# Retention projections as Strassen blocks, with weight sums made in DRAM by transfers and the heads' outputs projected at the end

## The chip, the cores and the metric

One core of one Trainium2 chip. The metric is the device time of one execution in microseconds, as the median of several. The operands are float32; TensorE (PE) multiplies them as pairs of a rounded high part and a remainder ("hi" and "lo", type float32r), three matmuls for one: hi x hi, hi x lo, lo x hi. PE takes matmuls in the order in which they stand in its queue, as the other engines do with theirs.

## The reference

Two layers over 528 tokens (16 learned ones and 512 of the input) of width 1024. Layer 0 is retention and a SwiGLU FFN, layer 1 a gated DeltaNet and another FFN. The change is in the retention, which is, for 4 heads (q and k 256 wide, v and gate 512 wide):

```python
proj = h @ w_in                        # q, k, v, g of all heads
q = rope(q, pos); k = rope(k, pos)
scores = einsum("bhid,bhjd->bhij", qc, kc) * dmask
o = scores @ vc + (qc * xi) @ state    # chunkwise, with a decaying state
o = o * rsqrt(mean(o * o) + eps) * gn_w * silu(g)
h = h + o @ w_out
h = h + swiglu(rmsnorm(h, ffn_norm_w), w_gate, w_up, w_down)
```

The kernel works without chunks: it forms all scores of a head with the decay as a mask.

## The kernel before

Everything is kept transposed: `h` holds 8 tiles of 128 features by 528 tokens (`KT` = 8, `T` = 528), and a projection multiplies a 128x128 block of weights, held fixed in PE, with 264 columns of tokens, twice for the two halves. A tile of 128 outputs takes 8 such blocks x 3 matmuls x 2 halves = 48 matmuls (`gemm`, `mm3`, line 308). Weights come as 128x1024 float32 (512 KB) through the SP queue into `wraw`, and ScalarE (ACT) and VectorE (DVE) split them into `whi` (line 165) and `wlo` (line 166).

`retention` goes head by head: four tiles of q and k, rotated by `rope` (DVE, lines 425 to 427, split at 298 and 299) as soon as each pair of tiles is there; four tiles of v; four of the gate g; and four weight tiles of the projection of the head's output (`out_proj`), which runs among the next head's q and adds to `h` (line 417). So each head has 16 weight tiles and 768 matmuls of 264 columns. Scores (`ret_scores`), the transposition of v by token (`ret_values`) and the attending (`ret_attend`) are generators that `tick` takes a step further after every few matmuls of a projection, so that they stand among them in PE's queue. The normalisations run through `row_rsqrt`: squares summed by tiny matmuls (lines 390, 392), DVE makes `rc` (397), GpSimd (POOL) takes the power -1/2 (398), PE spreads it over partitions (401, 405), ACT copies it to `rb` (409, 410).

The FFNs do most of their first projections as Strassen blocks already (`forms`, `strassen`): a 2x2 block product with seven products in place of eight. `forms` makes seven combinations of the activations (names `fhb11` and so on, high and low), and `strassen` makes the weight sums on DVE (lines 275 to 286 and 269) before each product is split and multiplied.

The order on each engine is set by a scheduler: it lists each engine's instructions by the program's priority and by when it takes them to be ready. What it made of the change is shown below, with the change.

Of the kernel before, what the change touches and what calls it, by code (L numbers as in the profile page):

```python
# [14 lines left out]
P = 128  # L15
D = 1024
# [15 lines left out]
FORM = 3  # L32
PLAIN = 4
# [12 lines left out]
class Hybrid:  # L46
# [58 lines left out]
    def setup(self):  # L105
# [16 lines left out]
        for half in range(2):  # L122
            c = slice(half * 512, half * 512 + 512)
            nc.sync.dma_start(self.h[:, half, :], a["hT"][half])
            nc.sync.dma_start(self.first_w[0][:, c], a["w_qk"][0, 0, :, c])
# [4 lines left out]
        for kt in range(2, KT):  # L130
            nc.sync.dma_start(self.h[:, kt, :], a["hT"][kt])
            if kt == 4:
                nc.sync.dma_start(self.first_w[1], a["w_qk"][0, 1])
# [49 lines left out]
    FORMS = ("b11", "t1", "t2", "b22", "t3", "b21", "t4")  # L183

    def forms(self, st, fp, lo, hw):
# [6 lines left out]

        for k0 in (0, 2):
            f = self.t(fp, [P, 6 * hw], "wsum")
            a, b, c = (f[:, 2 * hw * i : 2 * hw * (i + 1)].rearrange("p (a b) -> p a b", a=2) for i in range(3))

            def block(dst, n, k0=k0):
                kb, half = 4 * (int(n[0]) - 1) + k0, int(n[1]) - 1
                cs = slice(lo + half * hw, lo + half * hw + hw)
                for k in range(2):  # L200
                    nc.vector.scalar_tensor_tensor(
                        dst[:, k, :], hh[:, kb + k, cs], g[:, kb + k : kb + k + 1], rb[:, cs], op0=ALU.mult, op1=ALU.mult
                    )

# [9 lines left out]
            yield FORM  # L214
            parts("b11", a)
            block(c, "22")
            yield FORM
            minus(a, b, a)
            parts("t1", a)
            minus(b, c, b)  # L220
            yield FORM
            minus(a, c, a)
            parts("b22", c)
            yield FORM
            parts("t2", a)
            block(c, "21")
            yield FORM
            parts("t3", b)
            minus(a, c, a)
            yield FORM  # L230
            parts("b21", c)
            parts("t4", a)
            yield FORM

    def quad(self, src, sp):
# [7 lines left out]
    def strassen(self, raw, st, sp, hw, out):  # L243
# [34 lines left out]
        nc.vector.tensor_tensor(s, s, raw["11"], op=ALU.subtract)  # L278
        product(s, "t2", xb, False)
        c22 = taken(zs)  # L280
        nc.vector.tensor_tensor(s, raw["12"], s, op=ALU.subtract)  # L281
# [4 lines left out]
        nc.vector.tensor_tensor(raw["21"], raw["11"], raw["21"], op=ALU.subtract)  # L286
# [152 lines left out]
    def ret_scores(self, rp, dp, hd, q, k, km, out):  # L439
# [4 lines left out]
        nc.gpsimd.dma_start(dm[:96], a["decm"][:, hd, :])  # L444
        dr = self.t(dp, [P, NT], "dr")
        nc.gpsimd.dma_start(dr, a["decr"][:, hd, :])
# [5 lines left out]
        for c0, c1 in ((NM, T), (0, NM)):  # L452
# [11 lines left out]
            sc = self.t(dp, [P, NT], "sc")  # L464
# [5 lines left out]
        for j in range(4):  # L470
# [12 lines left out]
            sc = self.t(dp, [P, NT], "sc")  # L483
# [7 lines left out]
    def ret_values(self, rp, hd, x, rb, ready):  # L491

        nc, a = self.nc, self.a
        vhi = self.t(rp, [P, 4, 512], "vhi", F32R)
        vlo = self.t(rp, [P, 4, 512], "vlo", F32R)
        vm = self.t(rp, [P, 512], "vm", F32R)

        def by_token(v, vt):
# [16 lines left out]
        steps = []  # L515
        for v in range(4):
            w = ready.pop(0) if ready else self.load_w(a["w_v"][hd, v])
            p = self.psum_g()
            self.gemm(p, w, x, range(KT))
            vt = self.t(self.tp, [P, T], "ra", bufs=4)  # L520
            nc.vector.tensor_tensor(self.halves(vt), self.flat(p), self.halves(rb), op=ALU.mult)
            steps.append(self.spawn(by_token(v, vt), VT))
        steps.append(self.spawn(meta(), VT + 1))
        return (vhi, vlo, vm), steps

    def ret_attend(self, rp, v3, sc, oraw, out, steps):
# [6 lines left out]
        oacc = self.t(rp, [P, T], "oacc")  # L533
# [22 lines left out]
    def retention(self, st, ctx, nxt):  # L556
        nc, a = self.nc, self.a
        x = (st["hi"], st["lo"])
        rp = self.pool(ctx, "ret", 1)
        dp = self.pool(ctx, "retd", 2)  # L560
# [5 lines left out]

        def begin():
            for kt in range(KT):
                self.norm_square(st, kt)
                yield 1  # L570
                if kt == 3:
                    nc.sync.dma_start(cosr, a["cos"])
                    nc.sync.dma_start(sinr, a["sin"])
# [3 lines left out]
            yield 1  # L577

# [5 lines left out]
        left = lambda: None  # L584
        for hd in range(RH):
            qk = {}
            raw = []
            oraw = self.t(rp, [P, 4, T], "oraw") if hd == 0 else None
            for i, nme in enumerate("qk"):
                if hd + i == 0:  # L590
                    first = [self.psum_g() for half in range(2)]
                    self.gemm_pair(first, w0, x)
                for half in range(2):
                    if hd + i == 0:
                        p = first[half]
                    else:
                        w = self.load_w(a["w_qk"][hd, 2 * i + half])
                        p = self.psum_g()
                        self.gemm(p, w, x, range(KT))
                    p = p[:, :, :HH]  # L600
                    if hd == 0:
                        keep = self.halves(oraw[:, 2 * i + half, :])
                        nc.scalar.copy(keep, p)
                        p = keep
                    raw.append(p)
                    if i == 0 and half == 0:
                        left()
                hi = self.t(rp, [P, 2, T], nme + "hi", F32R)
                lo = self.t(rp, [P, 2, T], nme + "lo", F32R)
                qk[nme] = (hi, lo)  # L610
                if hd > 0:
                    self.rope(hi, lo, raw[2 * i], raw[2 * i + 1], cosr, sinr)
            ready = []
            if hd == 0:
                ready = [self.load_w(a["w_v"][0, v]) for v in range(2)]
                self.finish(rows)
                rb = st["rb"]
                for i, nme in enumerate("qk"):
                    self.rope(*qk[nme], raw[2 * i], raw[2 * i + 1], cosr, sinr)
            sc = {}  # L620
            scores = self.spawn(self.ret_scores(rp, dp, hd, qk["q"], qk["k"], km, sc), SCORES[hd > 0])
            v3, steps = self.ret_values(rp, hd, x, rb, ready)
            self.finish(scores)
            if hd == 0:
                self.late_consts()
            else:
                oraw = self.t(rp, [P, 4, T], "oraw")
            orow = {}
            attend = self.spawn(self.ret_attend(rp, v3, sc, oraw, orow, steps), TO_ATTEND)
            ohi = self.t(rp, [P, 4, T], "ohi", F32R)  # L630
            olo = self.t(rp, [P, 4, T], "olo", F32R)

            def gated(v, sg, oraw=oraw, orow=orow, ohi=ohi, olo=olo):
                nc.vector.scalar_tensor_tensor(
                    oraw[:, v, :], oraw[:, v, :], self.gnw[:, v : v + 1], orow["rb"], op0=ALU.mult, op1=ALU.mult
                )
                nc.vector.tensor_tensor(sg, sg, oraw[:, v, :], op=ALU.mult)
                self.split(ohi[:, v, :], olo[:, v, :], sg)

            sgs = []  # L640
            for v in range(4):
                w = self.load_w(a["w_g"][hd, v])
                p = self.psum_g()
                self.gemm(p, w, x, range(KT))
                sg = self.t(self.tp, [P, T], "ra", bufs=4)
                nc.vector.tensor_tensor(self.halves(sg), p[:, :, :HH], self.halves(rb), op=ALU.mult)
                nc.scalar.activation(sg, sg, AF.Silu)
                sgs.append(sg)
                if v == 1:
                    self.finish(attend)  # L650
                if v > 0:
                    gated(v - 1, sgs[v - 1])
            gated(3, sgs[3])

            def out_proj(hd=hd, og=(ohi, olo), nst=None):
                for mp in range(4):
                    w = self.load_w(a["w_ro"][hd, mp])
                    for mi in range(2):
                        p = self.psum_g()
                        self.gemm(p, w, og, range(4), off=mi * 512)  # L660
                        self.add_h(p, 2 * mp + mi)
                        if nst:
                            self.norm_tile(nst, 2 * mp + mi)

            left = out_proj
        nst = nxt()
        out_proj(nst=nst)
        return nst

    def ffn_hidden(self, layer, st, lo, fp, up, name):  # L670
# [13 lines left out]
        for jp in range(PLAIN // 2):  # L684
            raw = self.quad(a["w_gu"][layer, jp], up)
# [40 lines left out]
        for jp in range(PLAIN // 2, FT // 2):  # L726
            raw = self.quad(a["w_gu"][layer, jp], up)

            def out(row, half, gate, u, jp=jp):
# [5 lines left out]
                nc.scalar.activation(s, gate, AF.Silu)  # L735
                own = j - 2 * KT + PLAIN
                dst = s if own >= PLAIN else late[j // KT][:, j % KT, cs]
                nc.vector.tensor_tensor(dst, s, u, op=ALU.mult)
# [706 lines left out]
def _layout(v):  # L1445
# [16 lines left out]
    q, k = blocks(w[:, :1024]), blocks(w[:, 1024:2048])  # L1462
    o["w_qk"] = c(np.concatenate([q.reshape(RH, 2, P, D), k.reshape(RH, 2, P, D)], axis=1))
    o["w_v"] = c(blocks(w[:, 2048:4096]).reshape(RH, 4, P, D))
    o["w_g"] = c(blocks(w[:, 4096:]).reshape(RH, 4, P, D))
    o["w_ro"] = c(
# [75 lines left out]
```

## Time and profile before

| what | us |
|---|---|
| median of 3 executions (1735.25 to 1739.01) | 1735.62 |
| the profiled execution | 1738.03 |
| its span, first to last instruction | 1736.2 |
| PE busy (matmul) | 1712.2 |
| DVE busy | 1138.5 |
| ACT busy | 802.6 |
| POOL busy | 74.6 |

The profile comes from one execution. A row of the timeline or of the chain gives start, duration, engine, line, operation and operands (out<-in), and how often; what is in brackets is the idle time before and what ended it. PE's matmuls overlap a little, so the spacing between them, not the length of one, is what a stretch costs. A row of a window gives its length and each engine's busy time with the number of instructions, then PE's granted clock, the busy share of the 16 transfer engines, and GB/s.

### The profile page before, as it was taken

What the parts mean: (1) busy time and instruction counts of PE and PEld (TensorE: products, weight loads), DVE (VectorE), ACT (ScalarE), POOL (GpSimd) and SP (SyncE); (2) the same over time, 40 slices, a digit from 0 to 9 for tenths busy, and PEclk for the clock granted to TensorE, in tenths of its full rate; (3) what the DMA queues carried; (4) which work ended last, traced back from release to release, by engine and by line L of the source; (5) the groups of instructions that cost most, each with busy time, mean ns of one, the idle gap of its engine ahead of it and who ended that gap; (6) DMA issues with size and microseconds to landing.
All of it is one profiled execution on the core that took longest, in us unless ns stands there. A gap on an engine that the chain in (4) does not pass through costs nothing.

```text
span 1736.2 us, 30593 instructions
## 1 busy us (share of the span) xinstructions
PE 1712.2 (99%) x12671; PEld 1598.5 (92%) x12671; DVE 1138.5 (66%) x1789; ACT 802.6 (46%) x1451; POOL 74.6 (4%) x138
## 2 busy tenths in 40 slices
PE   9999999999999999999999999999999999999997
PEld 8999999999999999999989978787877889999886
DVE  6555455554798777633588786685858798887322
ACT  5322322323444544523465526765666545445422
POOL 1000000000000000000030000000001000000010
PEclk9999999999999999999999999999999999999999
DMA  6222122221323322333255453433322223333221
GB/s 200 85 74 96 62 86 74 69 78 61 118 68 107 98 98 86 101 89 92 94 189 164 128 160 124 149 98 113 108 91 86 97 77 117 100 98 98 97 96 62
DMA packets 78747, 177.32 MB, mean 102 GB/s; under 512 B 19296, under 2 KB 36880, under 8 KB 78608
## 3 DMA queue, kind: packets, MB, share of 16 engines
q1 hardware_dynamic: 70704, 170.87, 30.7%
q0 software_dynamic: 944, 2.66, 0.5%
q10 hardware_dynamic: 6960, 1.84, 0.5%
q8 instruction: 99, 1.62, 0.4%
q14 instruction: 40, 0.33, 0.1%
HBM read 157.50 MB, written 17.84 MB: 101 GB/s over the span
## 4 chain that ended last, share of the span: by engine, by line
PE 87%; DVE 5%; issue 5%; ACT 2%; DMA 1%; POOL 0%; SPq 0%; POOLq 0%; ACTq 0%; DVEq 0%
PE g L308 72%; PE m L308 9%; DVE wlo L299 1%; DVE wlo L166 1%; DVE ra L799 1%; DMA sraw<-in_w_gu_dram 1%; PE m L405 1%; DMA h<-in_hT_dram 0%; ACT whi L298 0%; PE m L1124 0%; PE m L502 0%; PE m L392 0%; PE m L948 0%; ACT whi L165 0%; PE m L1225 0%
## 5 line engine op out<-in xcount | busy, mean ns | idle before, releaser
L308 PE MATMUL g<-xhi,whi 128*128 128x264 f32 (+1 forms) x1600 | 377.9, 305 | 1.3 <-ACT xhi L361 1.3
L308 PE MATMUL g<-xhi,wlo 128*128 128x264 f32 (+1 forms) x1600 | 366.0, 299 | 2.0 <-DVE wlo L166 2.0
L308 PE MATMUL g<-xlo,whi 128*128 128x264 f32 (+1 forms) x1600 | 365.8, 299 | 1.2 <-DVE xlo L362 1.2
L165 ACT CAST whi<-wraw 128x1024 fp32r<-128x1024 f32 (+1 forms) x176 | 181.1, 1030 | 378.6 <-PE g L308 308.0
L166 DVE TENSOR_TENSOR wlo<-wraw,whi 128x1024 fp32r<-128x1024 f32 (+1 forms) x176 | 210.7, 1199 | 163.5 <-ACT whi L165 159.0
L308 PEld LDWEIGHTS g<-xhi,whi 128*128 128x128 f32 x1600 | 256.9, 189 | 12.3 <-ACT xhi L361 2.0
L308 PEld LDWEIGHTS g<-xhi,wlo 128*128 128x128 f32 x1600 | 256.1, 189 | 10.7 <-DVE wlo L166 2.2
L308 PEld LDWEIGHTS g<-xlo,whi 128*128 128x128 f32 x1600 | 256.1, 189 | 8.7 <-DVE xlo L362 2.0
L308 PE MATMUL g<-fht,whi 128*128 128x264 f32 (+1 forms) x576 | 163.8, 284 | 0.2 <-DVE ra L269 0.2
L308 PE MATMUL g<-fht,wlo 128*128 128x264 f32 (+1 forms) x576 | 162.7, 282 | 0.6 <-DVE wlo L299 0.6
L308 PE MATMUL g<-flt,whi 128*128 128x264 f32 (+1 forms) x576 | 163.2, 283 | 0.0
L308 PEld LDWEIGHTS g<-fht,wlo 128*128 128x128 f32 x576 | 109.0, 189 | 0.9 <-DVE wlo L299 0.9
L308 PEld LDWEIGHTS g<-fht,whi 128*128 128x128 f32 x576 | 108.1, 188 | 0.9 <-issue 0.6
L308 PEld LDWEIGHTS g<-flt,whi 128*128 128x128 f32 x576 | 108.2, 188 | 0.0
L299 DVE TENSOR_TENSOR wlo<-wsum,whi 128x1024 fp32r<-128x1024 f32 x54 | 66.1, 1225 | 37.6 <-ACT whi L298 37.6
L298 ACT CAST whi<-wsum 128x1024 fp32r<-128x1024 f32 x54 | 56.6, 1048 | 72.7 <-DVE wsum L281 33.8
L308 PE MATMUL g<-fhb,wlo 128*128 128x264 f32 (+1 forms) x288 | 81.4, 283 | 0.5 <-DVE wlo L299 0.5
L308 PE MATMUL g<-fhb,whi 128*128 128x264 f32 (+1 forms) x288 | 81.8, 284 | 0.0
L308 PE MATMUL g<-flb,whi 128*128 128x264 f32 (+1 forms) x288 | 81.6, 283 | 0.0
L799 DVE SCALAR_TENSOR_TENSOR ra<-pad,convw,ra 128x528 f32<-128x528 f32 x96 | 75.4, 786 | 5.7 <-ACT ra L797 4.9
L417 DVE TENSOR_TENSOR h<-h,g 128x528 f32<-128x528 f32 x40 | 28.1, 703 | 53.0 <-PE g L308 53.0
L298 ACT CAST whi<-sraw 128x1024 fp32r<-128x1024 f32 x44 | 46.2, 1050 | 34.3 <-PE g L308 32.0
(397 smaller groups left out, 3721.9 us busy)
## 6 DMA issues: line engine op xcount, KB each, us to landing
wraw<-in_w_gu_dram SPq DMA_DIRECT2D x44, 512.0 KB, 3.3
sraw<-in_w_gu_dram SPq DMA_DIRECT2D x44, 512.0 KB, 3.5
wraw<-in_w_d_dram SPq DMA_DIRECT2D x38, 512.0 KB, 3.5
wraw<-in_w_v_dram SPq DMA_DIRECT2D x16, 512.0 KB, 3.3
wraw<-in_w_g_dram SPq DMA_DIRECT2D x16, 512.0 KB, 3.4
wraw<-in_w_ro_dram SPq DMA_DIRECT2D x16, 512.0 KB, 3.4
wraw<-in_w_dqk_dram SPq DMA_DIRECT2D x16, 512.0 KB, 3.4
wraw<-in_w_dv_dram SPq DMA_DIRECT2D x16, 512.0 KB, 3.4
```

Source lines behind the costliest of these rows:

```text
L165: nc.scalar.copy(hi[:, c], raw[:, c])
L166: nc.vector.tensor_tensor(lo[:, c], raw[:, c], hi[:, c].bitcast(F32), op=ALU.subtract)
L298: self.nc.scalar.copy(hi, src)
L299: self.nc.vector.tensor_tensor(lo, src, hi.bitcast(F32), op=ALU.subtract)
L308: mm(o, l, r[which], start=first and n == 0, stop=last and n == 2, **kw)
L405: nc.tensor.matmul(pr[:, j * P : (j + 1) * P], rc[:, j + 1 : j + 2].to_broadcast([P, P]), self.ident, start=True, stop=True)
L417: self.nc.vector.tensor_tensor(hs, hs, ps[:, :, :HH], op=ALU.add)
L799: nc.vector.scalar_tensor_tensor(acc, pad[:, i : i + T], cw[:, mt, i : i + 1], acc, op0=ALU.mult, op1=ALU.add)
```

## The change

Of the twelve projections of 1024 outputs (four heads; q with k, v, and g), nine become blocks of seven products (`quad`). Three stay plain (`plain`): q with k of head 0 and the gates of heads 0 and 1, which run first, while `forms` makes the seven combinations of the normalised activations. The gates of heads 0 and 1 go to DRAM (`d_sg`) until they are wanted.

The sums of weights that the blocks need are made before their use in DRAM. `sums` issues, on GpSimd's queue, plain copies and transfers that add to what stands at their destination (`accum_op=ALU.add`, in pieces of 1024 bytes): eight of 512 KB per block, 72 in all, each add behind the copy that it builds on. Because a transfer can only add here, signs move from the weight sums into the activations (`neither` in `forms`) and the results, in the FFNs too, where the sums stay on DVE. `all_sums` issues a step of it every 8 ticks from the moment the row factor `rb` of the first normalisation is there: a tiny transfer from `rb` to each `s1` puts that in order.

A block's outputs are gathered in SBUF. There is no room beside the combinations, so the first normalised activations (`xhi`, `xlo`) and `h` itself serve as space after `forms`, `h` is loaded again from its input, the heads' gated outputs go to DRAM (`d_o`) and come back, and their projection runs at the end over all four heads, in two passes of four output tiles, each followed by the next norm's `norm_tile`. The tables dm and dr, which GpSimd fetched, now come through SP.

```diff
-    def forms(self, st, fp, lo, hw):
+    def forms(self, st, fp, lo, hw, temp=None, pause=None):
...
+    def sums(self, w, s):
+
+        dma = self.nc.gpsimd.dma_start
+        dma(s["s1"], w[1])
+        dma(s["s3"], w[0])
+        yield
+        dma(s["s1"], w[2], accum_op=ALU.add, max_dma_last_dim=ROW)
+        dma(s["s3"], w[1], accum_op=ALU.add, max_dma_last_dim=ROW)
+        yield
+        dma(s["s2"], s["s1"])
+        yield
+        dma(s["s2"], w[0], accum_op=ALU.add, max_dma_last_dim=ROW)
+        yield
+        dma(s["s4"], s["s2"])
+        yield
+        dma(s["s4"], w[3], accum_op=ALU.add, max_dma_last_dim=ROW)
+
+    def quad(self, w, s, forms, hw, rows, tick=None):
...
+        def product(name, form, banks, first):
+            hi, lo = self.load_w(src[name])
+            fh, fl = forms[form]
+            for i in range(2):
+                for k in range(4):
...
+        product("11", "b11", xb, True)
+        nc.scalar.copy(t0[:, :, left], xs)
+        product("s1", "t1", zb, True)
+        nc.scalar.mul(t1[:, :, right], zs, -1.0)
+        product("s2", "t2", xb, False)
+        nc.scalar.copy(t0[:, :, right], xs)
+        product("s4", "b22", zb, False)
+        add(t0[:, :, right], zs)
+        product("s3", "t3", xb, False)
+        add(t1[:, :, right], xs, ALU.subtract)
+        yb = [self.psum_m()[:, :hw] for _ in range(2)]
+        product("12", "b21", yb, True)
+        for i in range(2):
+            add(t0[:, i, left], yb[i])
+        product("22", "t4", xb, False)
+        nc.scalar.mul(t1[:, :, left], xs, -1.0)
...
+        def all_sums():
+            rb = st["rb"]
+            gens, left = [], list(quads)
+            n = 0
+            while gens or left:
+                if left and n % SUMS_APART == 0:
+                    q = left.pop(0)
+                    nc.gpsimd.dma_start(sums[q]["s1"][:1, :4], rb[:1, :4])
+                    gens.append(self.sums(w[q[0], q[1]], sums[q]))
+                for g in list(gens):
+                    if next(g, True):
+                        gens.remove(g)
+                n += 1
+                yield SUMS_PAUSE
...
+        def roped(hd):
+            product(hd, QK, ct)
+            for i, nme in enumerate("qk"):
+                self.rope(*qk[nme], self.halves(ct[:, 2 * i, :]), self.halves(ct[:, 2 * i + 1, :]), cosr, sinr)
...
+        for hd in range(1, RH):
+            qk = qk_tiles()
+            roped(hd)
+            if hd < 3:
+                self.finish(attend)
+                stored(hd - 1, orow)
+            sc = scored(hd)
...
+            orow, steps, attend = attended(hd, *sc)
```

The first place where the order matters is GpSimd's queue around the power of head 0's normalisation. Before, it stands here (rc_00174, the first is that of the layer's norm, rc_00045; dm and dr are heads' decay tables):

```order
L398 TENSOR_TENSOR rc_00045_288<-rc_00045_288,mhalf_00012_115 128x5
L387 MEMSET rc_00719_5076 128x5
L444 DMA dm_00409_2876<-in_decm_dram 96x528
L446 DMA dr_00410_2878<-in_decr_dram 128x512
L398 TENSOR_TENSOR rc_00174_989<-rc_00174_989,mhalf_00012_115 128x5
```

After, the same power (rc_00313) stands here; in d_s431, 4 is the sum s4, 3 the head and 1 its kind (0 for q and k, 1 for v, 2 for g), rows of 16x8192 are copies, those of 512x256 add:

```order
L262 DMA d_s430_00047_175<-in_w_ret_dram 512x256
L258 DMA d_s231_00050_178<-in_w_ret_dram 512x256
L253 DMA d_s132_00053_181<-in_w_ret_dram 512x256
L254 DMA d_s332_00056_184<-in_w_ret_dram 512x256
L260 DMA d_s431_00051_179<-d_s231_00050_178 16x8192
L256 DMA d_s232_00054_182<-d_s132_00053_181 16x8192
L463 MEMSET rc_00849_5217 128x5
L262 DMA d_s431_00051_179<-in_w_ret_dram 512x256
L258 DMA d_s232_00054_182<-in_w_ret_dram 512x256
L260 DMA d_s432_00055_183<-d_s232_00054_182 16x8192
L474 TENSOR_TENSOR rc_00313_1640<-rc_00313_1640,mhalf_00012_115 128x5
```

Two small transfers stood ahead of it; now 71 of the 72 large ones do, the last three links of them each waiting for the one before. PE's steps that need this rc (lines 477 and 481) stand in the q/k block of head 1, in its fifth product, and have 852 matmuls of 264 columns ahead of them.

The second place is DVE's queue where head 1 passes from q and k to v. Before, with the rotation at 425 to 427 and the splitting of v's weights at 166 (here head 2, where the rows are the same):

```order
L425 TENSOR_TENSOR ra_2834<-g_2728,cosr_157 128x528
L425 TENSOR_TENSOR ra_2835<-g_2728,sinr_158 128x528
L166 TENSOR_TENSOR wlo_2981<-wraw_2978,whi_2980 128x1024
L425 TENSOR_TENSOR ra_2836<-g_2783,sinr_158 128x528
L425 TENSOR_TENSOR ra_2837<-g_2783,cosr_157 128x528
L426 TENSOR_TENSOR ra_2834<-ra_2834,ra_2836 128x528
L427 TENSOR_TENSOR ra_2835<-ra_2835,ra_2837 128x528
L166 TENSOR_TENSOR wlo_3059<-wraw_3056,whi_3058 128x1024
```

After, in head 1 (h_73 holds the block's outputs, wlo_1851 belongs to v's first product, wlo_1902 to its second; ahead of these rows stand the four products of q with the tables):

```order
L503 TENSOR_TENSOR ra_1809<-ra_1809,ra_1811 128x528
L745 SCALAR_TENSOR_TENSOR h_73<-h_73,gnw_504,rb_1718 128x528
L501 TENSOR_TENSOR ra_1822<-h_73,cosr_200 128x528
L375 TENSOR_TENSOR qlo_1425<-ra_1808,qhi_1424 128x528
L375 TENSOR_TENSOR qlo_1425<-ra_1809,qhi_1424 128x528
L501 TENSOR_TENSOR ra_1823<-h_73,sinr_201 128x528
L501 TENSOR_TENSOR ra_1824<-h_73,sinr_201 128x528
L501 TENSOR_TENSOR ra_1825<-h_73,cosr_200 128x528
L502 TENSOR_TENSOR ra_1822<-ra_1822,ra_1824 128x528
L503 TENSOR_TENSOR ra_1823<-ra_1823,ra_1825 128x528
L748 TENSOR_TENSOR xlo_1103<-xlo_1103,h_73 128x528
L375 TENSOR_TENSOR klo_1427<-ra_1822,khi_1426 128x528
```

The splitting of v's weights, which stood between the steps of the rotation, has moved behind all of them: three rows further on comes wlo_1851.

More of the change, by code (lines that the diff above doesn't have):

```diff
@@ new lines, in quad, with add @@
+    def quad(self, w, s, forms, hw, rows, tick=None):
+        nc = self.nc
+        src = {**s, **dict(zip(self.BLOCKS, (w[i] for i in range(4))))}
+        t0, t1 = rows
+        left, right = slice(0, hw), slice(hw, 2 * hw)
+        x, z = self.psum_g(), self.psum_g()
+        def product(name, form, banks, first):
[3 more added lines that the diff above has]
+                for k in range(4):
+                    ws = slice(i * 512 + k * P, i * 512 + (k + 1) * P)
+                    self.mm3(
+                        [banks[i]],
+                        (hi[:, ws], lo[:, ws]),
+                        [(fh[:, k, :], fl[:, k, :])],
+                        first and k == 0,
+                        k == 3,
+                        skip_group_check=True,
+                    )
+                    if k % 2:
+                        self.tick()
+        def add(dst, ps, op=ALU.add):
+            nc.vector.tensor_tensor(dst, dst, ps, op=op)
+        xb, zb = [x[:, i, :hw] for i in range(2)], [z[:, i, :hw] for i in range(2)]
+        xs, zs = x[:, :, :hw], z[:, :, :hw]
+        product("11", "b11", xb, True)
[14 more added lines that the diff above has]
+        nc.scalar.mul(t1[:, :, left], xs, -1.0)
@@ L513, in meta @@
             yield 1
[L515 to L524, printed above, removed]
+        return [self.spawn(by_token(v), VT + v) for v in range(4)] + [self.spawn(meta(), VT + 4)]
     def ret_attend(self, rp, v3, sc, oraw, out, steps):
@@ L565, in retention, with tables @@
         sinr = self.t(rp, [P, T], "sinr")
+        def tables():
+            nc.sync.dma_start(cosr, a["cos"])
+            nc.sync.dma_start(sinr, a["sin"])
         def begin():
@@ L582, in retention @@
         nc.gpsimd.memset(self.vms, 0.0)
[L584 to L588, printed above, removed]
-            for i, nme in enumerate("qk"):
[L590 to L595, printed above, removed]
-                    else:
[L597 to L665, printed above, removed]
@@ L666, in retention, with plain @@
-        nst = nxt()
-        out_proj(nst=nst)
+        def plain(hd, kind, row, ws=None):
+            if ws is None:
+                ws = [self.load_w(w[hd, kind, u]) for u in ((0, 3), (1, 2))[row]]
+            ps = [self.psum_g() for _ in range(2)]
+            for kts in (range(4), range(4, EARLY), range(EARLY, KT)):
+                for i in range(2):
+                    off = i * 512 + (kts[0] % 4) * P
+                    self.gemm(ps[i], ws[kts[0] // 4], x, kts, kts[0] == 0, kts[-1] == KT - 1, off=off)
+            return ps
@@ new lines, in qk_tiles @@
+        def qk_tiles():
+            return {n: [self.t(rp, [P, 2, T], n + s, F32R) for s in ("hi", "lo")] for n in "qk"}
+        qk = qk_tiles()
+        with ExitStack() as c:
+            ep = self.pool(c, "reth", 1)
+            keep = self.t(ep, [P, 4, T], "keep")
+            for row in range(2):
+                for i, p in enumerate(plain(0, QK, row, w0 if row == 0 else None)):
+                    nc.scalar.copy(self.halves(keep[:, 2 * row + i, :]), p[:, :, :HH])
+            self.finish(rows)
+            for i, nme in enumerate("qk"):
+                self.rope(*qk[nme], self.halves(keep[:, 2 * i, :]), self.halves(keep[:, 2 * i + 1, :]), cosr, sinr)
@@ new lines, in retention @@
+        self.late_consts()
+        tables()
+        self.spawn(all_sums())
+        rb = st["rb"]
+        fo = self.pool(inner, "retf", 1)
+        prepared = self.spawn(
+            self.forms(st, fo, 0, HH, lambda: [self.t(dp, [P, T], n, bufs=b) for n, b in (("dm", 1), ("dr", 1), ("sc", 2))], FORM_RET), 1
+        )
+        for hd in range(2):
+            for row in range(2):
+                for i, p in enumerate(plain(hd, G, row)):
+                    sg = self.t(self.tp, [P, T], "ra", bufs=4)
+                    nc.vector.tensor_tensor(self.halves(sg), p[:, :, :HH], self.halves(rb), op=ALU.mult)
+                    nc.scalar.activation(sg, sg, AF.Silu)
+                    nc.sync.dma_start(d_sg[hd][:, 2 * row + i, :], sg)
@@ new lines, in retention, with product, scored @@
+        self.finish(prepared)
+        xv = self.t(self.xp, [P, KT, T], "xhi", F32R)
+        xt = self.t(self.xp, [P, KT, T], "xlo")
+        vm = self.t(rp, [P, 512], "vm", F32R)
+        v3 = (xv[:, 0:4, :NT], xv[:, 4:8, :NT], vm)
+        at, bt, ct, oraw = xt[:, 0:4, :], xt[:, 4:8, :], self.h[:, 4:8, :], self.h[:, 0:4, :]
+        def product(hd, kind, rows):
+            self.quad(w[hd, kind], sums[hd, kind], st["forms"], HH, (rows[:, 0:2, :], rows[:, 2:4, :]))
+        def scored(hd):
+            sc = {}
+            return sc, self.spawn(self.ret_scores(rp, dp, hd, qk["q"], qk["k"], km, sc), SCORES[hd > 0])
@@ new lines, in stored, with gate, reload @@
+        def stored(hd, orow):
+            for v in range(4):
+                gated(orow, v)
+            nc.sync.dma_start(d_o[hd], bt)
+        def gate(hd):
+            product(hd, G, bt)
+            for r in range(2):
+                g = bt[:, 2 * r : 2 * r + 2, :]
+                nc.scalar.activation(g, g, AF.Silu)
+        nc.sync.dma_start(bt, d_sg[0])
+        sc = scored(0)
+        orow, steps, attend = attended(0, *sc)
+        for hd in range(1, RH):
+            qk = qk_tiles()
+            roped(hd)
[3 more added lines that the diff above has]
+            sc = scored(hd)
+            if hd == 1:
+                nc.sync.dma_start(bt, d_sg[1])
+            orow, steps, attend = attended(hd, *sc)
+            if hd > 1:
+                if hd == 3:
+                    first = qk_tiles()
+                    def reload():
+                        for step in steps:
+                            self.finish(step)
+                        nc.sync.dma_start(at, d_o[0])
+                        yield 4
+                        for i, n in enumerate("qk"):
+                            self.split(*first[n], at[:, 2 * i : 2 * i + 2, :])
+                    reloaded = self.spawn(reload(), TO_ATTEND)
+                gate(hd)
+                self.finish(attend)
+                if hd == 2:
+                    stored(hd, orow)
```

187 lines of the change are left out of this document (143 added, 44 removed).

## The prediction

> **What bounds the kernel now.** I read the page first, then PE's waits in the retention stage, then the chain of work there and in the first FFN, then GpSimd's timeline. The page:
>
> ```profile
> span 1736.2 us, 30593 instructions
> PE 1712.2 (99%) x12671; PEld 1598.5 (92%) x12671; DVE 1138.5 (66%) x1789; ACT 802.6 (46%) x1451; POOL 74.6 (4%) x138
> ...
> L166 DVE TENSOR_TENSOR wlo<-wraw,whi 128x1024 fp32r<-128x1024 f32 (+1 forms) x176 | 210.7, 1199 | 163.5 <-ACT whi L165 159.0
> ```
>
> PE's own waits from 0 to 480 us, which is the retention stage and the start of the first FFN:
>
> ```profile
> PE g L308 <- ACT xhi L361: 1.3, 3, 0.5
> PE g L308 <- DVE xlo L362: 1.2, 4, 0.3
> PE m L129 <- DVE ones L118: 1.1, 1, 1.1
> ```
>
> All three belong to the first 14 us. After that PE waits for nobody until the stage is over: here a matmul less is time less, and any new wait of PE is time more. Nothing hides it.
>
> The price of a matmul comes from the chain in order of time (start, us, what). First the values of head 2 before, then five Strassen blocks of the first FFN:
>
> ```profile
> 278.82 5.84 PE g L308 x48
> 284.66 0.44 PE m L502 x4
> ...
> 576.62 17.81 PE g L308 x144
> 594.43 2.92 PE m L308 x24
> 597.35 17.72 PE g L308 x144
> ...
> 679.88 14.69 PE g L308 x119
> ```
>
> 48 matmuls of 264 columns take 5.84 us, 0.122 each; a plain 1024x1024 product, four such tiles, takes 4 x 5.84 = 23.4 us. Five Strassen products (168 matmuls each) fill 679.88 - 576.62 = 103.3 us, 20.65 each. The same `forms` and the same shape of product serve the change.
>
> **The change part by part.** *Fewer matmuls.* Nine of twelve projections become seven block products: 9 x (23.4 - 20.65) = 24.8 us less on PE. The projection at the end has the same 768 matmuls in another order, the scores and the attending are the same. The heads' outputs go to DRAM and back and h is loaded again; h is wanted only about 40 us later, when the first pass's sums are whole, and wo's first two tiles (96 matmuls, 11.7 us) need head 0 alone, which is loaded ahead. I cost these at nothing; were the load of head 1 late, it would be a few us. The FFN's changed signs keep the number and shape of its operations: nothing.
>
> *The sums in DRAM.* For each of nine blocks GpSimd issues four copies of 512 KB from DRAM to DRAM and four transfers that add 512 KB to what is there: 72 in all. They stand in its queue in order, each add behind the copy that it builds on. The order puts the `pow` of head 0's normalisation (rc_1640) behind all of them but the last (the rows are above). PE's two steps that take that rc stand in the middle of head 1's q/k block, and PE takes its instructions in order: whatever the chain of sums lasts beyond that point, PE stands still. Before, the same `pow` had only tiny neighbours:
>
> ```profile
> 2.83 0.54 POOL L444 DMA_DIRECT2D dm<-in_decm_dram  x1
> ...
> 25.95 1.20 POOL L398 TENSOR_TENSOR rc<-rc,mhalf 128x5 f32<-128x5 f32 x1 [14.71 <-DVE am L381]
> ...
> 89.12 1.21 POOL L398 TENSOR_TENSOR rc<-rc,mhalf 128x5 f32<-128x5 f32 x1 [30.42 <-DVE rc L397]
> ```
>
> *When PE gets there.* PE's timeline has it 138 matmuls of 264 columns in at
>
> ```profile
> 30.37 0.49 PE L308 MATMUL g<-xhi,whi 128*128 128x264 f32 x2
> ```
>
> and after the change 852 stand ahead of that place: 714 x 0.122 = 87.1 us. Scores, transposes and attending come on top, from the chain (head 2 before):
>
> ```profile
> 269.64 4.55 PE m L308 x24
> ...
> 274.80 0.71 PE m L308 x6
> ...
> 276.24 0.62 PE m L308 x6
> ...
> 307.24 0.24 PE m L543
> 307.48 1.85 PE m L308 x12
> ```
>
> 5.9 for the scores, five transpositions of 0.44 (2.2), about 8.7 for four times 0.24 + 1.85 and the start of it, 1.2 for the first normalisation: 30.4 + 87.1 + 18.0 = 135.5 us, if PE never waits before.
>
> *How long the chain of sums lasts.* No transfer of before goes from DRAM to DRAM or adds. The nearest rows, line by line KB and us to landing, and the whole stretch of PE's work with DMA share and GB/s at its end:
>
> ```profile
> wraw<-in_w_v_dram SPq DMA_DIRECT2D x16, 512.0 KB, 3.3
> dr<-in_decr_dram POOLq DMA_DIRECT2D x4, 256.0 KB, 4.9
> fnw<-in_fnw_dram POOLq DMA_DIRECT2D x1, 512.0 KB, 4.5
> ...
> 14.34:476.00 461.66, 461.31 (x3655) 453.12 (x3656) 261.03 (x403) 157.37 (x230) 9.32 (x14) 1.00 0.26 84
> ```
>
> Lower bound: by dependence. From the moment the first row factor is there (about 31 us) some 18 to 19 links must land one after another before `pow`; at 4.5 us each it is due at 33 + 19 x 4.5 = 119 us, in time. But that lets the engines carry any number at once. By their capacity: 84 GB/s at a share of 0.26 is 323 GB/s when full, so 512 KB occupy all 16 for 1.62 us. Of the 71 transfers ahead of `pow` the last need only be issued; to be carried are 35 copies (35 x 1.62 = 57 us) and 35 adds. An add reads two blocks and writes one where a copy reads one and writes one; three passes for two make 1.5 x 1.62 = 2.43 us, 85 us in all. The weights hold 0.26 of the engines meanwhile, so (57 + 85) / 0.74 = 192 us, and from the first copy at 6 us on `pow` is free at 198. An add as cheap as a copy gives 6 + 114 / 0.74 = 160; one at twice the price 6 + 171 / 0.74 = 237. I take 198, the middle, as an estimate: PE goes on at 199, a wait of 199 - 135.5 = 63.7 us.
>
> The Trainium skill, Collectives: The Full Stack, section "The bandwidth ceiling: the fold count and why AG ≠ RS ≠ AR", says that an add inside the transfer engine halves the rate because it needs two source reads; no run here shows it yet, and by it `pow` comes at the upper of these ends, which is a rival below. The skill's DMA: Bandwidth & Descriptors, section "Latency and other measured facts", has copies between DRAM tensors at 207 to 214 GB/s, an estimated 2.45 us per 512 KB, which would push the sum to about 1835 us as well (35 x 2.45 + 85 in place of 57 + 85); that too no run here shows.
>
> *DVE's queue between q/k and v.* Before, the rotation's steps alternate with the splitting of weights (`wlo`). Now q and k come out of their block only at its end, and from the rows above v's first `wlo` stands behind the whole rotation. DVE's steps on 528 columns follow each other every 0.62 us, and PE is not waiting:
>
> ```profile
> 258.55 0.71 DVE L425 TENSOR_TENSOR ra<-g,cosr 128x528 f32<-128x528 f32 x1 [0.94 <-PE g L308]
> ...
> 259.17 0.70 DVE L425 TENSOR_TENSOR ra<-g,sinr 128x528 f32<-128x528 f32 x1
> ...
> 256.28 1.32 DVE L299 TENSOR_TENSOR qlo<-ra,qhi 128x528 fp32r<-128x528 f32 x2
> ...
> L634 DVE SCALAR_TENSOR_TENSOR oraw<-oraw,gnw,rb 128x528 f32<-128x528 f32 x16 | 11.9, 766 | 0.0
> ```
>
> From the first product with cosr to that `wlo`: 12 steps x 0.62, two pairs of lows at 1.32, two gatings at 0.77, an addition and a gate product (about 1.0), the `wlo` at 1.2 = 13.8 us. The first can start some 3.4 us before PE ends the block; PE wants the `wlo` 0.5 us after. So PE waits 13.8 - 3.4 - 0.5, about 10 us, after the q/k blocks of heads 1 and 2. In head 3 no gating is due and two `wlo` stand further ahead: about 2. Together 22 us, nearly the whole gain. The same happens once in head 0 (rotation and first forms, some 31 steps of which 25 at 0.62, ahead of a `wlo`): about 6 us, and the copies that GpSimd now issues among the first loads may cost 2. These last two fall before PE's place at 135.5 and vanish in the wait there.
>
> **Sum.** -24.8 + 63.7 + 22 = +61 us. The profiled execution took 1738.0 us, 1.8 beside its span and 2.4 above the median of 1735.6; the difference is carried to the median: 1797 us.
>
> **The rivals.**
>
> *The sums are in time* (18 in 100). If DRAM-to-DRAM transfers overlap as the 4.5 us links allow, `pow` is free before PE comes at 135.5 + 6 + 2 = 143.5, and only DVE's queue costs: -24.8 + 8 + 22 = +5, 1741 us. It decides where `pow` is free before 143. For it: half of the engines' time is unused here (share 0.26). Against: 70 transfers in some 137 us would need (143 - 6) x 0.74 / 70 = 1.45 us each, less than a plain load occupies.
>
> *Only the count of matmuls shows* (8 in 100): the sums are in time and DVE's work stays beside PE's, as it does before, so that no `wlo` is late: -24.8, 1711 us, the other side of no change. For it: before, DVE is busy 261 of 462 us and PE never waits. Against: the rows of the order. It needs the rotation to be 10 us shorter than its steps' durations add up to.
>
> *Each add costs two transfers or more* (17 in 100): `pow` at 237 us, PE on at 238, a wait of 102.5: -24.8 + 102.5 + 22 = +100, 1835 us, and more if pieces of 1 KB are dearer than the loads' 4 KB rows. The skill's rule named above is this one.
>
> *Gain and waits cancel* (5 in 100): about 1736, which needs `pow` in time and half of DVE's wait.
>
> The forecast, a wait of PE of 25 to 90 us for the `pow` behind the sums, has 52 in 100.
>
> **How the numbers follow.** Differences under 0.2% (3.5 us) can't be told from none. Faster holds the second rival, 0.08; same 0.05 from the last; slower is the rest, 0.52 + 0.18 + 0.17 = 0.87. The range starts just below the first rival, 1739, which leaves out the faster case and part of "same", and ends at 1858, above the 1835 of two reads per add, leaving out a few in 100 with dearer pieces.
>
> **What would show it.** Right: PE's longest wait stands near 135 to 145 us at line 477 or 481 (m from rc), ends near 200 us, and GpSimd's `pow` of that rc comes right before it; the add transfers land one after another until then, with the DMA share far above 0.26 from 10 to 200 us; PE waits about 10 us for `wlo` at line 170 after the q/k blocks of heads 1 and 2; Strassen blocks without a wait take 20.65 us. Wrong: `pow` runs as soon as DVE's rc is written; or weights from the sums land late and PE waits there instead; or the block after q/k starts without a gap; or a block takes much more than 20.65 us with the operands there.

## The result and the profile after

The changed kernel took 1826.78 us (median of 4, 1824.29 to 1833.2) where the kernel before took 1735.43 beside it: ratio 1.0527 (95% interval 1.0497 to 1.0557), 91.3 us slower. Forecast were 61 us more, 1797, with a range from 1739 to 1858. The profiled execution took 1833.2, its span 1831.3.

The page of the changed kernel, its head and slices (each digit a fortieth of the span, 46 us):

```profile
span 1831.3 us, 30532 instructions
PE 1705.7 (93%) x12455; PEld 1589.7 (87%) x12455; DVE 1174.3 (64%) x1840; ACT 854.9 (47%) x1518; POOL 132.0 (7%) x211
PE   8984077999999999999999999999999999999997
DMA  9999852554523233233325446243233233332321
```

PE stands still in the fifth slice, and until then the transfer engines are full. What it waited for from 0 to 600 us is in its waits, of which these are the six largest (engine, line, waited for: us in total, times, longest):

```profile
PE m L477 <- POOL rc L474: 71.8, 2, 66.5
PE g L384 <- DVE wlo L170: 18.7, 3, 8.4
PE g L384 <- DVE ra L715: 4.4, 2, 2.3
PE g L384 <- ACT xlo L295: 3.6, 1, 3.6
PE g L384 <- ACT h L309: 2.6, 2, 1.3
PE g L384 <- ACT xhi L437: 2.4, 1, 2.4
```

The long one is for head 0's `rc`, the forecast's place. GpSimd's own rows just before it ends, and PE's first row behind it:

```profile
206.93 0.52 POOL L260 DMA_DIRECT2D d_s<-d_s  x1 [5.16 <-DMA d_s<-in_w_ret_dram]
...
214.68 1.03 POOL L258 DMA_DIRECT2D d_s<-in_w_ret_dram  x1 [0.16 <-issue]
223.46 0.52 POOL L260 DMA_DIRECT2D d_s<-d_s  x1 [7.75 <-DMA d_s<-in_w_ret_dram]
223.99 1.23 POOL L474 TENSOR_TENSOR rc<-rc,mhalf 128x5 f32<-128x5 f32 x1
```

```profile
225.27 0.60 PE L477 MATMUL m<-ident,rc 16*128 16x16 f32 x2 [66.51 <-POOL rc L474]
```

The two copies shown waited 5.16 and 7.75 us (in brackets) for the adds that they build on, and `pow` runs at once behind the last copy that stands ahead of it. PE had arrived at 225.3 - 66.5 = 158.8. From the chain that ended last, the end of head 1's rotation, behind which v's `wlo` and then PE's matmuls come:

```profile
244.03 1.24 DVE klo L375 x2
...
245.94 1.15 DVE wlo L170
...
247.13 5.09 PE g L384 x22
```

Nearly all of the difference has arisen by the end of the retention: a stretch of 371 matmuls at the start of the first FFN begins at 479.68 before (first row) and at 572.80 after (second), 93.1 us of the 95.1 by which the spans differ, and takes the same time.

```profile
479.68 45.36 PE g L308 x371
```

```profile
572.80 45.34 PE g L384 x371
```

### The profile page after: what moved, and what is told of

Same layout as the page of the kernel before. It is cut to its first block, busy times and chain, and to the rows that moved or that the text cites. A ratio compares the mean times of both kernels' runs of the same rounds, so it can differ in the third digit from the quotient of the medians.

```text
span 1831.3 us, 30532 instructions
## 1 busy us (share of the span) xinstructions
PE 1705.7 (93%) x12455; PEld 1589.7 (87%) x12455; DVE 1174.3 (64%) x1840; ACT 854.9 (47%) x1518; POOL 132.0 (7%) x211
## 3 DMA queue, kind: packets, MB, share of 16 engines
q0 software_dynamic: 20816, 38.55, 9.5%
## 4 chain that ended last, share of the span: by engine, by line
PE 73%; DMA 10%; DVE 7%; issue 6%; POOL 2%; ACT 2%; POOLq 0%; ACTq 0%; DVEq 0%
PE g L384 57%; PE m L384 11%; DMA d_s<-in_w_ret_dram 6%; DMA d_s<-d_s 2%; DMA d_s<-rb 2%; DVE wlo L170 1%; DVE wlo L375 1%; DVE ra L501 1%; DMA sraw<-in_w_gu_dram 1%; PE m L481 0%; ACT whi L374 0%; DVE ra L984 0%; PE m L1309 0%; PE m L1133 0%; ACT whi L169 0%
## 5 line engine op out<-in xcount | busy, mean ns | idle before, releaser
L170 DVE TENSOR_TENSOR wlo<-wraw,whi 128x1024 fp32r<-128x1024 f32 (+2 forms) x203 | 243.3, 1201 | 232.0 <-ACT whi L169 225.5
L169 ACT CAST whi<-wraw 128x1024 fp32r<-128x1024 f32 (+2 forms) x203 | 209.4, 1032 | 368.9 <-PE g L384 197.4
L384 PE MATMUL g<-xhi,whi 128*128 128x264 f32 (+1 forms) x1024 | 257.8, 316 | 6.8 <-DVE ra L715 4.4
L384 PE MATMUL g<-fht,whi 128*128 128x264 f32 (+1 forms) x864 | 249.7, 289 | 7.6 <-ACT xlo L295 3.6
L384 PE MATMUL g<-xhi,wlo 128*128 128x264 f32 (+1 forms) x1024 | 250.6, 310 | 2.0 <-DVE wlo L170 2.0
L384 PE MATMUL g<-xlo,whi 128*128 128x264 f32 (+1 forms) x1024 | 250.3, 309 | 0.0
L384 PE MATMUL g<-fht,wlo 128*128 128x264 f32 (+1 forms) x864 | 246.5, 285 | 2.7 <-DVE wlo L170 2.1
L384 PEld LDWEIGHTS g<-xhi,whi 128*128 128x128 f32 x1024 | 168.9, 192 | 17.2 <-DVE ra L715 4.8
L384 PEld LDWEIGHTS g<-xhi,wlo 128*128 128x128 f32 x1024 | 168.7, 192 | 11.3 <-DVE wlo L170 2.4
L384 PEld LDWEIGHTS g<-xlo,whi 128*128 128x128 f32 x1024 | 169.0, 192 | 6.9 <-DVE xlo L438 0.3
```

The source lines that it names most:

```text
L169: nc.scalar.copy(hi[:, c], raw[:, c])
L170: nc.vector.tensor_tensor(lo[:, c], raw[:, c], hi[:, c].bitcast(F32), op=ALU.subtract)
L384: mm(o, l, r[which], start=first and n == 0, stop=last and n == 2, **kw)
```

## The experiments

In all of them what is not named is as in the changed kernel. Ratios are to the kernel before on the same chip, with their 95% interval; times of runs on different chips are compared by these ratios. e2, e3 and e5 leave out work that the result needs, so they are probes and no replacements.

| run | what | us | ratio |
|---|---|---|---|
| changed kernel | | 1826.8 | 1.0527 (1.0497 to 1.0557) |
| e1 | power off GpSimd | 1767.1 | 1.0180 (1.0154 to 1.0206) |
| e2 | no sums | 1739.9 | 1.0015 (1.0003 to 1.0027) |
| e3 | copies for adds | 1786.3 | 1.0285 (1.0264 to 1.0306) |
| e4 | adds in pieces of 8 KB | 1814.7 | 1.0448 (1.0423 to 1.0474) |
| e5 | no sums, rotation among v's products | 1711.7 | 0.9864 (0.9846 to 0.9882) |
| e6 | e1 and that rotation | 1756.2 | 1.0109 (1.0082 to 1.0136) |
| e7 | all sums on DVE | 1757.1 | 1.0131 (1.0112 to 1.0151) |
| e8 | e7 and that rotation | 1742.3 | 1.0039 (1.0020 to 1.0057) |
| e9 | e6, head 0's v on DVE | 1746.6 | 1.0042 (1.0025 to 1.0058) |
| e10 | e9, adds in pieces of 8 KB | 1772.8 | 1.0198 (1.0184 to 1.0213) |
| e11 | e9, sums begun later | 1741.3 | 1.0018 (1.0009 to 1.0027) |
| e12 | e11, sums in DRAM for three blocks, on DVE for six | 1731.9 | 0.9969 (0.9956 to 0.9981) |

**e1: the power away from the queue.**

```diff
-        nc.gpsimd.tensor_tensor(rc, rc, self.mhalf.to_broadcast([P, 5]), op=ALU.pow)
+        nc.scalar.activation(rc, rc, AF.Sqrt)
+        nc.vector.reciprocal(rc, rc)
```

> In the retention the power -1/2 of the row factors is taken by ACT's square root and DVE's reciprocal; all sums stay as they are. Theory Q (the stop is the place in GpSimd's queue): PE's waits of 66.5 and 5.3 us for rc go, with about 3 us of slowly spaced matmuls behind them; the sums themselves are in time (by the order, those of head 1's v are through at about 113 us and wanted at about 160): 1826.8 - 66.5 - 5.3 - 3 = 1752 us. Theory L (the sums are late themselves): the wait moves to the weights loaded from the sums, some 60 us for wraw, whi or wlo in the blocks of heads 1 to 3, time 1815 us or more.

1767.1 us, 60 less, between theory Q (1752) and theory L (1815). Both waits for `rc` are gone, but one of 16.9 us stands in head 0's v (lines are one higher here):

```profile
PE g L385 <- ACT xlo L296: 16.9, 1, 16.9
```

The row names ACT's copy of a result; the chain that ended last shows what held ACT:

```profile
92.30 8.69 DMA d_s<-in_w_ret_dram
...
101.04 7.83 DMA wraw<-d_s
...
108.97 1.04 ACT whi L170
110.02 0.51 ACT xlo L296
...
110.57 6.34 PE g L385 x30
```

An add landed at 101.0, the sum was loaded in 7.8 us, and ACT, in order too, split it before the copy that PE waited for. So theory Q holds for the long stop and theory L for the first block alone. In the changed kernel the same sum was as late:

```profile
108.87 0.59 PE L384 MATMUL g<-fht,whi 128*128 128x264 f32 x1 [3.59 <-ACT xlo L295]
```

There PE came to this place only at 105.3, in e1 at 93.6, since it had waited before, 5.3 us of it for the first norm's `pow`. These earlier waits hid most of the lateness, and the long stop behind them took in the rest.

**e2: no sums.** `all_sums` isn't spawned.

> Leaves out all 72 transfers of the sums; the products load four input blocks of the same size in their place, and the power stays on GpSimd. Theory Q: 1826.8 - 66.5 - 5.3 - 3 as in the run without the power on GpSimd, and less what the full transfer engines cost PE in waits (3.6 + 2.4 + 1.3 us): about 1745 us. What is left above 1711 is then the queue of DVE after q and k. Theory C (full transfer engines slow all loads, and the wait for rc is only the last of it): 1725 us or less, over 20 us below the run with sums and no power on GpSimd.

1739.9 us, near theory Q's 1745 and not at theory C's 1725, but 27 below e1 on the same chip, which was theory C's other sign. So the sums cost some 27 us even where nothing waits for the power; e1's wait of 16.9 us is the largest part that its waits show. What is left, ratio 1.0015, is about what the prediction's first rival gave for sums that are in time (1741).

**e3 and e4: what an add costs.** e3 takes `accum_op=ALU.add` out of the four lines of `sums`; e4 is this:

```diff
-ROW = 1024
+ROW = 8192
```

> The 36 transfers that add become plain copies in the same pieces of 1024 bytes (the sums are not formed); queue and links as they are. In the changed kernel the 69 transfers between 20 and 240 us held all 16 engines for 2.43 us each on average. If an add is dear because it reads twice (copy 1.62, add 3.24): 35 x 1.62 / 0.77 = 74 us less, the power at about 150 us, hardly a wait, 1760 us. If the pieces of 1024 bytes are what is dear: power at about 224 us as before, 1827 us.

> The adding transfers go in pieces of 8192 bytes in place of 1024; all else as changed. If the pieces are what is dear: the power at about 150 us, hardly a wait, 1760 us. If an add is dear because it reads twice: power at about 224 us, 1827 us.

Neither theory alone: `pow` came at 180.4 in e3 and 208.5 in e4, against 224.0. And e3 changed two things, not one: its page counts 6,992 packets in GpSimd's queue where e4's has 4,688 and the changed kernel's 20,816, so its copies did not go in pieces of 1 KB. The queue's rows (packets, MB, share of the 16 engines' span) of the changed kernel, e3 and e4:

```profile
q0 software_dynamic: 20816, 38.55, 9.5%
```

```profile
q0 software_dynamic: 6992, 38.55, 6.0%
```

```profile
q0 software_dynamic: 4688, 38.55, 8.0%
```

Times their spans (1831.3, 1781.8, 1812.4) that is 174, 107 and 145 us of all engines for 72 transfers. From these come three estimates, which take a copy to cost the same in all three runs, though e3's pieces have yet another size. A copy takes 107 / 72 = 1.48 us; an add takes (174 - 36 x 1.48) / 36 = 3.35 us in pieces of 1 KB and (145 - 53) / 36 = 2.55 in pieces of 8 KB. So an add costs about 1.7 copies, and small pieces raise that to 2.3. The Trainium skill, Collectives: The Full Stack, section "The bandwidth ceiling: the fold count and why AG ≠ RS ≠ AR", puts an add inside the transfer engine at two source reads and half the rate; 1.7 and 2.3 copies lie on either side of that.

In e4's profile `pow` came 16 us earlier and the span was 18.9 us shorter; the medians differ by 12. PE came to the stop later:

```profile
209.75 0.60 PE L477 MATMUL m<-ident,rc 16*128 16x16 f32 x2 [26.88 <-POOL rc L474]
```

That is 182.9 in place of 158.8: ahead of it PE had waited 6.9, 5.8 and twice up to 2.7 us for results that ACT, in order, copied only after splitting weights that were loaded late. Until PE's stop, SP's loads of weights landed in 11.8 us and those of finished sums in 15.2 (medians), where the changed kernel has 7.8 for both. PE's later arrival vanishes in the stop, of which only the end counts, but the larger pieces made SP's loads slower.

**e5 and e6: the rotation among v's products.** The rotation becomes a generator that yields after every step, the gating likewise; scores wait for it.

```diff
-SCORES = (12, 3)
+SCORES = (12, 17)
...
-                self.rope(*qk[nme], self.halves(ct[:, 2 * i, :]), self.halves(ct[:, 2 * i + 1, :]), cosr, sinr)
+                    yield from self.rope_steps(
+                        *qk[nme], self.halves(ct[:, 2 * i, :]), self.halves(ct[:, 2 * i + 1, :]), cosr, sinr
+                    )
+            return self.spawn(steps())
```

> As the run without sums (the sums are left out, four input blocks are loaded in their place), and the rotation of heads 1 to 3 and the gating of heads 0 and 1 go step by step among v's products in place of ahead of them; scores start 17 ticks into v in place of 3. Theory D (DVE's queue between q/k and v costs what the count of matmuls gains): PE's waits for wlo (18.8 us) go, and with each of the three the 14 to 18 matmuls spaced 0.22 in place of 0.122 us behind it (1.5 us each): 1739.9 - 18.8 - 4.5 = about 1717 us. Rival (DVE is full there, the steps only displace others): wlo, sc or vm are late in the middle of v instead, 1735 to 1745 us.

> The full sums in DRAM, the power taken off GpSimd as before, and the rotation among v's products. Theory D: 1767.1 - 23 = 1744 us, and what stays above the run without sums is the lateness of the first block's sums (16.9 us at 110 us) and the full transfer engines. Rival: 1762 us or more, the waits of PE only move.

e5 took 1711.7 us. It moves three things, the rotation, the gating and the start of the scores. All that PE waits for in its first 600 us:

```profile
PE g L384 <- DVE ra L728: 2.7, 1, 2.7
PE m L133 <- DVE ones L122: 1.1, 1, 1.1
PE g L384 <- DVE wlo L170: 0.6, 2, 0.3
```

From e2 to e5 the ratio falls by 0.0151, 26 us: theory D, and a little more than the 23 expected. In e6, with the sums, the same edit brought 12 (1.0180 to 1.0109), half of it: the rotation's waits left, but PE then waited 19.5 us for the first block's sums, and 3.1 and 4.0 for copies of results in later blocks.

**e7 and e8: the sums on DVE**, from blocks loaded once more, in `quad`:

```diff
+            if name == "s1":
+                x, y = loaded("21"), loaded("22")
+                for t_, c in zip(s, cols):
+                    nc.vector.tensor_tensor(t_, x[:, c], y[:, c], op=ALU.add)
```

> The whole computation; the sums are made on DVE as in the FFN, from blocks loaded once more where needed (nine loads a block in place of seven), no transfers between DRAM tensors; rotation ahead of v as in the changed kernel. DVE gets 4 x 1.25 = 5 us more per block of 20.65. Theory (DVE has room, 42 of 60 us busy without sums): as without sums, 1740 us, and some 2 us more after each rotation since the sum for s1 stands behind it too: 1746 us. Rival (DVE becomes the bound): 9 x 5 = 45 us more, 1785 us.

> The whole computation, sums on DVE, rotation and gating among v's products. If DVE has room: the waits for wlo go, 1746 - 22 = about 1722 us, faster than before (1738) by about what the count of matmuls is worth less 8 us. If DVE is full: 1745 us or more.

1757.1, between the two theories, and 1742.3, near the one that DVE is full (1745 or more). DVE is not the bound throughout, but things of its come late: PE waits 10.1 us for a `wlo` twice in e7, and up to 4.8 for the `whi` of a split; in e8 3.3 us twice for a head's k (`kmh`), 4.0 in three waits for v by token (`vm`) and seven times up to 0.7 for a sum's `wlo`.

**e9 to e12: which sums where.** e9 leaves head 0's v out of `quads` and makes its sums on DVE; e10 adds `ROW = 8192`; e11 has this:

```diff
-SUMS_APART = 2
+SUMS_APART = 4
```

> The whole computation: power off GpSimd, rotation among v's products, and the sums of the first block (head 0's v), which came 19.5 us late, on DVE; the other eight blocks' sums in DRAM in pieces of 1024 bytes. If the late first block is most of what the sums still cost: 1756.2 - 19.5 - 2 = 1735 us, about as before. If the full transfer engines make the next sums late instead, PE waits in head 1's q/k block and it stays over 1745 us.

> As the run with the first block's sums on DVE, and the adding transfers in pieces of 8192 bytes, which held the engines for 2.0 in place of 2.4 us each on average: the sums are through about 25 us earlier. If the engines' time decides: 1725 us, faster than before. If plain loads of weights wait behind the larger pieces (with them PE waited more often for copies of late weights): 1740 us or more.

> As the run with the first block's sums on DVE, pieces of 1024 bytes, and a new block's sums begun every 4 in place of 2 steps, so that an early block's chain is done before later ones fill the engines. If the order of the blocks is what makes the sums late: 1728 us. If the sum of the transfers decides: as the run without pacing, or later blocks come late and it is slower.

e9 gained 12 us over e6 by the ratios, half of the 21 expected: the wait of 19.5 us is gone, but one of 6.5 us for a `whi` of the same block took its place, and 2.6, 2.4 and 1.8 for late loads or copies stand elsewhere. (These are of the profiled execution, 1739.0 us; the others took 1745 to 1749.) e11 is 5 us better than e9, where the order of the blocks was to bring it to 1728, and the wait for the `whi` is still there (6.6). e10 is 26 us worse. In e10, transfers between 20 and 240 us (KB, median us from issue to landing):

```profile
wraw<-in_w_ret_dram SPq DMA_DIRECT2D x26, 512.0 KB, 9.3
...
d_sg<-ra SPq DMA_DIRECT2D x8, 264.0 KB, 18.2
```

and in e9, with pieces of 1 KB:

```profile
wraw<-in_w_ret_dram SPq DMA_DIRECT2D x26, 512.0 KB, 7.5
...
d_sg<-ra SPq DMA_DIRECT2D x8, 264.0 KB, 7.5
```

The adds got cheaper (9.0 in place of 10.8 us to landing), and these transfers of SP slower; loads of finished sums, which in e4 were slower too, were not (4.8 in place of 6.8). PE's waits in its first 600 us came to 43 us in e10 and to 21 in e9. The Trainium skill, DMA: Bandwidth & Descriptors, section "Queues, rings and completion order", has each engine take turns between queues by the packet. That a queue with larger packets gets more of each turn would fit the slower loads and stores, but no run here varies the loads' own packets, so this cause is argued and not shown.

The last run keeps sums in DRAM only where DVE has no room:

```diff
-        quads = [(0, V), (1, QK), (1, V), (2, QK), (2, V), (2, G), (3, QK), (3, V), (3, G)]
+        quads = [(1, V), (2, V), (3, V)]
```

> The whole computation: power off GpSimd, rotation among v's products; sums in DRAM only for the v blocks of heads 1, 2 and 3, where the rotation takes DVE (24 transfers in place of 72, a new block's begun every 4 steps), and on DVE for the other six blocks. If DRAM sums cost by filling the transfer engines and DVE sums by crowding the rotation, each is now where there is room: 1720 us, some 12 behind the run with no sums at all (1711.7) and faster than before by 0.8%. If the waits only spread over more places: 1735 us or more.

1731.9 us, ratio 0.9969 (0.9956 to 0.9981): 0.3% less time than the kernel before, where 0.8% was expected, and nearer to the theory that the waits only spread (1735) than to the other (1720). No single wait is above 2.7 us (the first two rows of its waits are below), and by its windows (of the numbers at the end the last but one is the transfer engines' share) the engines are full only until about 100 us:

```profile
PE m L653 <- DVE vm L638: 3.1, 4, 2.1
PE g L417 <- ACT whi L407: 2.7, 1, 2.7
```

```profile
46.00:100.00 54.00, 50.53 (x397) 49.79 (x396) 37.84 (x63) 22.67 (x34) 9.16 (x12) 0.97 1.10 306
100.00:160.00 60.00, 55.92 (x416) 53.92 (x417) 44.09 (x75) 30.69 (x49) 0.00 (x0) 0.97 0.44 145
```

## Why the prediction was right, and where its sizes were off

The ratios split the 91 us. With 1736 us for the kernel before: the count alone (e5) is -0.0136, -23.6 us; DVE's queue (e2 over e5) +0.0151, +26; the sums beside the stop (e1 over e2) +0.0165, +29; the power's place (the changed kernel over e1) +0.0347, +60. Together +91, which holds by construction, as each run stands in two terms. Each ratio is uncertain by some 0.002, so each term by a few us. The split depends on the order too: taken with the sums there, the rotation's edit was worth 12 and not 26 (e6).

- **Fewer matmuls: -24.8 forecast, -23.6 measured.** e5 is the kernel of the second rival (1711), which needed DVE's work to stay beside PE's and the sums to cost nothing. The out-projection, the reloads and the FFN's signs at nothing: right, by PE's waits and the equal stretches above.
- **The power behind the sums: the place and the mechanism were right** (longest wait at line 477, `pow` directly behind the last transfers ahead of it, transfer engines full until then), and e1 shows it by taking the power out of that queue: 60 us. The length was near too, 66.5 for 63.7, but that was luck, by two errors that cancel: PE came at 158.8 in place of 135.5, and went on at 225.3 in place of 199. With a stop on the path only its end counts, and that end is 26 of the missing 30 us.
- **The term that was mis-sized is the price of an add**: "three passes for two make 1.5 x 1.62 = 2.43 us". By the estimates above it is 3.35, of which the pieces of 1 KB make 0.8; a copy is 1.48 where 1.62 was taken. The prediction's own formula with these, 6 + 35 x (1.48 + 3.35) / 0.74 = 234, comes out above the measured 224, since while PE stands hardly any weights are loaded: from 20 to 240 us the loads' queue held 22.9% of the engines, not 26, and with that the formula gives 6 + 169 / 0.77 = 225. From 160 to 224 us the sums' queue and that of the loads held

```profile
q0 software_dynamic: 7509, 12.31, 95.8%
q1 hardware_dynamic: 288, 1.05, 4.5%
```

of the engines. The third rival had the price: two copies or more for an add, `pow` at 237, 1835 us; the result lies closer to it (8 us) than to the forecast (30 us). The rule of two reads (the Trainium skill, Collectives: The Full Stack, the section named above) spoke for it, and the rival got 17 in 100. The other figure taken from the Trainium skill (DMA: Bandwidth & Descriptors, section "Latency and other measured facts"), an estimated 2.45 us for a copy between DRAM tensors, is not what this kernel shows (1.48).
- **PE's arrival.** The rotation of head 0 and the start "vanish in the wait", the prediction said, and they do. But it was 23 us and not 8: the first norm's `pow` too stood behind adds (5.3 us), for the copies and adds of `s3` aren't tied to `rb` and started at 6 us; DVE, which had to wait for that norm before the rotation and the first forms, was late twice (4.4 at line 715); the first block's sum was late (3.6), and a load of h (2.4); and slow matmuls followed on waits (below).
- **The first rival's condition was too narrow.** It set "the sums are in time" against "the power is late". e1 has the power on time and still stands 27 us above e2; 16.9 of them are the wait in head 0's v, which wants a sum from 93.6 us on that lands at 101.0 and is loaded at 108.9. In the changed kernel PE's delays ahead of that place covered most of it. Against this rival the prediction said that half of the engines' time was unused; a share of 0.26 leaves three quarters, which changes neither its sum nor its condition.
- **DVE's queue: 22 forecast, 26 measured.** The waits for `wlo` are 18.7 us, as forecast (8.2 and 8.4 for "about 10", 2.1 for "about 2"); the rest is two waits of 1.3 us for `h` and the slow matmuls behind each wait for `wlo`, some 1.5 us each.

## What to carry to other kernels

An instruction that everyone waits for does not belong in a queue in which links of a long chain wait for each other, however short it is; when it is taken out, look for the next wait that it covered. Price transfers by the time for which they hold all engines, not by their latency, and an add as about two copies (1.7 to 2.3 here) until a run says otherwise. When an algorithm saves matmuls by giving results later, the work on the other engines comes in one piece at the end of a block: spread it over the next block before counting the saving.

## What the hardware showed that was not expected

After a wait PE can be slow for a while. Starts of consecutive matmuls of 264 columns behind the wait for v's `wlo` in head 2, changed kernel:

```profile
320.29 0.59 PE L384 MATMUL g<-fhb,wlo 128*128 128x264 f32 x1 [8.35 <-DVE wlo L170]
320.68 0.42 PE L384 MATMUL g<-fhb,whi 128*128 128x264 f32 x1
320.90 0.42 PE L384 MATMUL g<-flb,whi 128*128 128x264 f32 x1
...
323.54 0.33 PE L384 MATMUL g<-flb,whi 128*128 128x264 f32 x1
323.71 0.28 PE L384 MATMUL g<-fhb,wlo 128*128 128x264 f32 x1
323.83 0.28 PE L384 MATMUL g<-fhb,whi 128*128 128x264 f32 x1
```

They follow each other every 0.22 us for 3.2 us, with a granted clock of 0.50, and then every 0.12, with 0.99; in the long stop it was 0.52 (160 to 226 us). A wait of 8 us thus costs about 1.5 more, and that of 3.6 us in head 0's v was followed by as many slow matmuls. The Trainium skill, TensorE: Matmul & The Clock Gate, section "What's actually happening", has the clock halved after about 3.4 us without work and restored after as long with it. These two waits agree with that. Others do not: behind the waits of 16.9 us (e1) and 66.5 us the slow stretch lasted 5.4 and 6.1 us; the wait of 2.1 us in head 3 was followed by 1.3 us at the fast spacing and then by 3.4 us at a granted clock of 0.50 (412.4 to 415.8), while one of 2.7 us in e1 (until 52.3) was followed by none, 1.00 to 60 us. So these traces don't give the length of wait from which the clock falls.

On GpSimd the issue of an add of 1 KB pieces took 1.03 us, of a copy 0.52 (the rows above). And tiny transfers are not quick among full engines: the 16 bytes that tie a block's sums to `rb` took 13.7 us on the chain of the changed kernel.

```profile
160.97 13.69 DMA d_s<-rb
```
